# Two elementwise products of a state-space scan on another engine, and the first layer's modulation by wide matrix products

## The chip, the cores and the metric

The program runs on one core of a Trainium2 chip. The core has a matrix engine (TensorE, PE in the profile, with its weight loads as PEld), a vector engine (VectorE, DVE), an engine for activations and scaled copies (ScalarE, ACT), a general engine (GpSimd, POOL) and a queue that issues the DMAs (SyncE, SP). The metric is the device time of one execution in microseconds (us), lower is better. A comparison of two versions of this kernel can tell about 0.3% from no change.

## The reference

Two layers of a diffusion backbone over 1024 latent tokens (x) and 256 context tokens, width 1024, fp32 in and out. Each layer does:

```python
mod = silu(c) @ w_mod[l] + b_mod[l]            # once for x (c), once for the context (c_ctx)
sh, sc, g = split(mod, 3)
h = rmsnorm(x, norm_w) * (1 + sc) + sh         # adaLN
fu, fg, q, k, v, ag, z, xbc, dt, gates = split(h @ w_in[l])
y_f = (fourier_mix(fu) * silu(fg)) @ w_of      # 2-D Fourier branch
y_a = (diff_attention(q, k, v) * silu(ag)) @ w_oa
y_s = rmsnorm(ssd(xbc, dt) * silu(z)) @ w_os   # bidirectional state-space (SSD) branch
x = x + g * ((sigmoid(g0)*y_f + sigmoid(g1)*y_a + sigmoid(g2)*y_s) @ w_out[l])
```

and the SSD branch, for chunks c of 128 tokens, 2 groups of 4 heads of 64 channels, state 128, both directions:

```python
y[c] = (C B^T * decay mask * dt) x + (C @ H_fwd[c]) * ecs_f + (C @ H_bwd[c]) * ecs_b + d_skip * x
H[c+1] = H[c] * etot[c] + B^T @ (x * w)        # the same backwards for H_bwd
```

The result is a final rmsnorm of x.

## The kernel before

All products of the model run on TensorE. Activations and weights are split into a high and a low fp16 part, so one product of the model is three fp16 matmuls of up to 512 columns; small products of the SSD scan, the transposes and the modulation are fp32, which the profile shows as two PE records for one matmul. Weights come as 512 KB halves into a ring of two raw buffers, are squared on ACT, given a power-of-two scale through a one-column product on PE, and are split by ACT and DVE into the w buffers. Activations live in 28 slots of SBUF (`ar`).

The builder writes the program as five cooperating threads: p (the projections of h), m (the three branches one after another: Fourier, attention, SSD), f (the merges with gates and w_out, and the norm of the next layer), e (the gates of the last branch) and g (the modulation of layer 1 and the residual gates). Every instruction goes to a list scheduler (`Scheduler.add` and `Scheduler.step`, lines 235 and 330), which keeps a planned clock for each engine, with a planned duration (`cost`, line 214) and planned delays between engines, and gives each engine that becomes free the ready instruction with the best priority. The priority is the number in order of creation, minus a bias by thread (`BIAS`, line 47). `AHEAD` says how many instructions a thread may have pending, `HOLD` when ACT and DVE may wait a little for a more urgent instruction, and the threads draw on common slots, PSUM banks and w buffers. The order that comes out is fixed at build time: on the chip each engine goes through its list in order and waits where an operand is late. So a change of a table, of a planned duration or of a dependency reorders the whole program.

All instructions are emitted at line 400, so the profile's rows have L400 throughout, and are told apart by engine, operation and tile.

The parts that the change touches:

- `mod0` (line 735) forms shift and scale of layer 0, before anything else can start. The modulation weights come as 16 tiles of 128 x 1024 (`in_wm`). For each tile 8 matmuls take 128 columns of the tile as stationary operand and the two columns of `cs` (silu of c and of c_ctx) as moving operand, all summed into 32 columns of one PSUM bank. Between the tiles the loads of x and of the first weights are issued. Then `modT` is read out, `mod_finish` makes `ab` of it, and `norm_T` transposes the first four tiles of x and applies `ab`; the first fp16 product needs all of that.
- `ssd_scan` (line 1280) runs per layer and group. Backwards first, 9 steps (`step`, line 1292): xw = x * w on DVE, one product on PE, then `new = old * etot` and `new += product`, both on DVE. Then for each chunk forwards: the mask from `rows`, C B^T on PE, ACT and DVE make the weighted mask, four products of 64 columns (`y`), C times both states (`y2`), and the sum on DVE, which begins with the skip product `acc = x * d_skip` and goes on with `acc += y` and so on. Then one `step` of H.
- When both groups are through, `ssd_out` norms and transposes the result to `zS`, and `merge_last` and `finish` follow, which need it whole.

Of the kernel before, what the change touches and what calls it, by code (L numbers as in the profile page):

```python
# [15 lines left out]
ALU = mybir.AluOpType  # L16
# [27 lines left out]
NSLOT = 28  # L44
NW = 8
RAW = 2
BIAS = {'m': 1200, 'p': 300, 'w': 1000, 'f': 0, 'e': -50000, 'g': -100000}
AHEAD = {'m': 120, 'p': 120, 'f': 40, 'e': 27, 'g': 6}
MAXB = {'m': 4, 'p': 3, 'f': 3, 'e': 1, 'w': 1, 'g': 1}
LEAST = (1, 1)  # L50
WLIM = {'p': 2, 'f': 4, 'e': 1}
# [1 line left out]
CAP = {'F': 5, 'S': 10, 'A': 9}  # L53
RES = 2
BOR, BMAX = 2, 4
HOLD = 0.25
X_AT, W_AT = 4, 7
G_AFTER = 'fu2'
F_START, F_FIN = 1000, 300
C_FIN = (2, 2)  # L60
# [90 lines left out]
class Scheduler:  # L151
# [66 lines left out]
    def cost(self, eng, name, outs, ins, kw, args):  # L218
        n = max(a.free_size() for a in outs + ins)
        if eng == 'PE':  # L220
            if name != 'matmul':
                return args[1].free_size() * NS_PE * 2 + 3.0
            n = args[2].free_size() * NS_PE
            return max(3.0 + n, 25.0) if ESIZE[ins[0].dtype] == 2 else max(4 * n + 3.0, 223.0)
        if eng == 'ACT':
            aps = len(ins) - 1
            return (51 if ins[0].space == PSUM else 93) + n * NS_ACT + 93 * (aps + len(outs) - 1)
        if eng == 'DVE':
            fast = name == 'tensor_copy' or name == 'tensor_scalar'
            fast = fast and all(a.space != PSUM for a in outs + ins)  # L230
            scal = sum(a.free_size() == 1 for a in ins[1:]) if name in ('tensor_scalar', 'scalar_tensor_tensor') else 0
            return 68 + n * NS_DVE * (0.5 if fast else 1) + 61 * scal
        return 60.0 if name != 'tensor_copy' else 150.0 + 2 * n

    def add(self, eng, name, fn, args, kw):
        o = Op()
# [181 lines left out]
class Builder:  # L418
# [173 lines left out]
    def prefetch(self, want=None):  # L592

        idle = self.block.get('f') in {(l, 'z' + b) for l in range(2) for b in ORDER[1:]}
        for k in 'pef' if idle else 'pfe':
            while self.wnext[k] and self.wnext[k][0][0] < (self.layers if k == 'p' else min(self.layers, self.flayer + 1)):
                l, name = self.wnext[k][0]
                ahead = k == 'p' and self.wnext['f'] and l > self.wnext['f'][0][0]
                left = k == 'f' and self.wnext['e'] and self.wnext['e'][0][0] == l
                lim = 1 if ahead else (0 if idle else 2) if left else WLIM[k] if (self.fetch_p if k == 'p' else self.fetch_f) else 0  # L600
                wo = name in ('wo0', 'wo1')
                need = 2 + max(0, self.later) + (0 if (l, name) == want else BOR if wo and self.wborrow < BMAX else 99)
                borrow = (ahead or wo) and len(self.free) >= need
                if not ahead and name[:2] != 'wo' and not self.later and (k != 'p' or l <= self.flayer) and self.spare < 4 and len(self.free) >= 6:
                    borrow = True
                if self.whold[k] >= lim or len(self.wfree) < 2 and not borrow:
                    break
                self.fetch(k)
# [126 lines left out]
    def mod0(self, L):  # L735

        nc, V = self.nc, self.nc.vector
        t = self.mm(True)
        nc.bias['w'] = 0
        zero = self.small(32)  # L740
        nc.gpsimd.memset(zero, 0.0)
        for k in range(8):
            for part in (1, 0):
                yield ('slots', 1)
                s = self.alloc()
                nc.sync.dma_start(s.v(1024), self.A['wm'][0, part, k])
                if k == 0 and part:
                    self.mul(t[:, 0:32], s.v(1024)[:, 0:128], zero, True, False)
                for b in range(8):
                    c = 16 * part + 2 * b  # L750
                    self.mul(t[:, c:c + 2], s.v(1024)[:, b * 128:b * 128 + 128], self.cs[:, k], False, k == 7 and not part and b == 7)
                s.drop()
            if k == 1:
                self.consts()
# [4 lines left out]
            if k == W_AT:  # L759
                self.fetch_p = True  # L760
                self.prefetch()
        modT = self.cst.tile([128, 16, 2], F32, name="modT0")
        V.tensor_tensor(modT, t[:, :32].rearrange("p (b s) -> p b s", s=2), self.pv[0][:, 0:16].unsqueeze(2).to_broadcast([128, 16, 2]), ALU.add)
        nc.close('p', True)
        self.mod_finish(L, modT)
        nc.bias['w'] = BIAS['w']
# [509 lines left out]
    def ssd_scan(self, L, g):  # L1276
# [14 lines left out]
        def step(c, dr, old, new):  # L1291
# [4 lines left out]
            if old is None:  # L1296
                V.tensor_copy(new, p[:, :256])
            else:
                V.tensor_tensor(new.rearrange(h4, q=64), old.rearrange(h4, q=64), bc4(L.etot, c, dr), ALU.mult)
                V.tensor_tensor(new, new, p[:, :256], ALU.add)  # L1300

        order = [9, 8, 7, 6, 5, 4, 3, 2, 1, 0]
# [4 lines left out]
        for c in [8, 9, 0, 1, 2, 3, 4, 5, 6, 7]:  # L1307
            if c < L.nt:
# [30 lines left out]
                if c != 9:  # L1339
                    self.mul(y2[:, 0:256], G.CT.v(1284)[:, o:o + 128], hb[c], True, True)  # L1340
                acc, t = self.scr()[:, :256], self.scr()[:, :256]
                V.tensor_tensor(acc.rearrange(h4, q=64), G.x[c].rearrange(h4, q=64),
                                b[:, 32 + g * 4:36 + g * 4].unsqueeze(2).to_broadcast([128, 4, 64]), ALU.mult)
                V.tensor_tensor(acc, acc, y[:, 0:256], ALU.add)
                for dr in range(2):
# [743 lines left out]
```

## Time and profile before

| | us |
|---|---|
| median of 3 runs | 2589.57 (2583.79 to 2592.41) |
| the profiled execution | 2585.78 |
| its span, first to last instruction | 2584.0 |
| PE busy | 2486.6 (96%) |
| DVE busy | 1821.3 (70%) |
| ACT busy | 1268.0 (49%) |
| POOL busy | 47.5 (2%) |

The program has no stage in which PE has nothing to do by design, so what counts is where PE stands idle, and where it runs at the lower of its two clocks. Both are read by stretches: idle is the length of a stretch minus PE's busy time in it, and PEclk is the clock that was granted (1.00 is 2.4 GHz, 0.50 is 1.2 GHz). Three stretches stand out from an even picture: the first 76 us, some 73 us near 2400 us, which are the last chunks of the second group's scan in layer 1 and `ssd_out`, and the last 14 us.

### The profile page before, as it was taken

What the parts mean: (1) busy time and instruction counts of PE and PEld (TensorE: products, weight loads), DVE (VectorE), ACT (ScalarE), POOL (GpSimd) and SP (SyncE); (2) the same over time, 40 slices, a digit from 0 to 9 for tenths busy, and PEclk for the clock granted to TensorE, in tenths of its full rate; (3) what the DMA queues carried; (4) which work ended last, traced back from release to release, by engine and by line L of the source; (5) the groups of instructions that cost most, each with busy time, mean ns of one, the idle gap of its engine ahead of it and who ended that gap; (6) DMA issues with size and microseconds to landing.
All of it is one profiled execution on the core that took longest, in us unless ns stands there. A gap on an engine that the chain in (4) does not pass through costs nothing. (4 is left out here: it accounts for less than half of the span.)

```text
span 2584.0 us, 42400 instructions
## 1 busy us (share of the span) xinstructions
PE 2486.6 (96%) x16800; PEld 1572.5 (61%) x16800; DVE 1821.3 (70%) x3823; ACT 1268.0 (49%) x2398; POOL 47.5 (2%) x93
## 2 busy tenths in 40 slices
PE   9999999999999999999999999999999999998698
PEld 9655665657565665575587556555655556556467
DVE  1868565687877898468956775776477768748766
ACT  2654453545655564456513654554464656446221
POOL 0200000000000000000000000000000000000000
PEclk9999999999999999999999999999999999999699
DMA  6132243354433334213722122434343423232331
GB/s 250 50 131 77 65 101 82 80 148 111 112 78 89 131 116 142 87 55 119 286 79 99 57 90 66 109 94 98 82 122 88 100 95 106 78 102 87 131 131 66
DMA packets 256979, 270.61 MB, mean 105 GB/s; under 512 B 181062, under 2 KB 191110, under 8 KB 256780
## 3 DMA queue, kind: packets, MB, share of 16 engines
q1 hardware_dynamic: 256780, 267.89, 34.5%
q8 instruction: 132, 2.16, 0.3%
q14 instruction: 67, 0.55, 0.1%
HBM read 178.02 MB, written 36.88 MB: 83 GB/s over the span
## 5 line engine op out<-in xcount | busy, mean ns | idle before, releaser
L400 PE MATMUL ps<-ar,w 128*128 128x512 f16 (+1 forms) x7296 | 1476.8, 355 | 3.7 <-ACT w L400 2.7
L400 PEld LDWEIGHTS <-w 128*128 128x128 f16 x7296 | 708.7, 98 | 649.6 <-issue 17.0
L400 PEld LDWEIGHTS <-ar 128*128 128x128 f16 x8000 | 648.9, 98 | 231.3 <-issue 26.4
L400 PE MATMUL ps<-ar,ar 128*128 128x128 f16 (+4 forms) x4564 | 564.7, 274 | 31.2 <-DVE ar L400 18.4
L400 PE MATMUL ps<-w,ar 128*128 128x256 f16 x3312 | 396.0, 273 | 0.0
L400 ACT ACTIVATE ar<-ps,s1m,qksc 128x1280 f32<-128x1280 f32 (+1 forms) x144 | 190.1, 1320 | 194.4 <-DVE s1m L400 158.0
L400 DVE TENSOR_REDUCE s1m<-ps 128x1 f32<-128x1280 f32 (+1 forms) x144 | 196.9, 1368 | 101.8 <-PE ps L400 91.0
L400 ACT ACTIVATE w<-raw 128x1024 f16<-128x1024 f32 x147 | 154.5, 1051 | 180.9 <-PE ps L400 105.5
L400 ACT ACTIVATE ar<-ar 128x1280 f16<-128x1280 f32 (+5 forms) x140 | 138.1, 987 | 104.6 <-DVE ar L400 103.0
L400 DVE TENSOR_TENSOR ar<-ar,ar 128x1280 f16<-128x1280 f32 (+3 forms) x116 | 123.4, 1064 | 9.3 <-ACT ar L400 9.0
L400 DVE SCALAR_TENSOR_TENSOR ar<-ar,pv,ar 128x1284 f32<-128x1284 f32 (+1 forms) x64 | 97.1, 1517 | 32.9 <-ACT ar L400 32.3
L400 ACT ACTIVATE ar<-ps 128x128 f32<-128x128 f32 (+5 forms) x192 | 67.3, 386 | 104.6 <-PE ps L400 103.6
L400 ACT ACTIVATE ar<-ps,ds 128x512 f32<-128x512 f32 (+1 forms) x86 | 53.9, 627 | 114.4 <-PE ps L400 114.3
L400 DVE SCALAR_TENSOR_TENSOR ar<-ar,s1m,ar 128x1280 f32<-128x1280 f32 (+1 forms) x72 | 103.1, 1432 | 0.0
L400 ACT ACTIVATE ar<-ar,ar 128x128 f32<-128x128 f32 x288 | 90.1, 388 | 22.8 <-DMA ar<-rows 21.7
L400 ACT ACTIVATE w<-raw,s1p 128x1024 f16<-128x1024 f32 x72 | 79.0, 1138 | 33.9 <-DVE s1p L400 33.7
L400 DVE SCALAR_TENSOR_TENSOR w<-raw,s1p,w 128x1024 f16<-128x1024 f32 x72 | 89.8, 1279 | 7.9 <-ACT w L400 7.7
L400 PE MATMUL ps<-k,ar 128*128 128x128 f32 (+1 forms) x492 | 79.3, 289 | 15.5 <-DVE ar L400 14.7
L400 DVE SCALAR_TENSOR_TENSOR w<-raw,s1f,w 128x1024 f16<-128x1024 f32 x65 | 81.4, 1279 | 9.8 <-ACT w L400 9.8
L400 PEld LDWEIGHTS ps<-k,ar 128*128 128x128 f32 x492 | 63.1, 157 | 38.2 <-DVE ar L400 23.3
L400 DVE SCALAR_TENSOR_TENSOR scrf<-ps,ds,ar 128x256 f32<-128x256 f32 x72 | 34.7, 482 | 72.6 <-PE ps L400 72.3
L400 PEld LDWEIGHTS ps<-ar,ar 128*128 128x128 f32 x428 | 67.0, 206 | 29.7 <-DVE ar L400 20.8
(218 smaller groups left out, 2157.0 us busy)
## 6 DMA issues: line engine op xcount, KB each, us to landing
raw<-in_wt SPq DMA_DIRECT2D x160, 512.0 KB, 4.7
ar<-in_wm SPq DMA_DIRECT2D x48, 512.0 KB, 6.4
ar<-rows SPq DMA_DIRECT2D x36, 512.0 KB, 4.5
yp<-scrf SPq DMA_DIRECT2D x64, 256.0 KB, 2.2
ar<-in_x SPq DMA_DIRECT2D x20, 512.0 KB, 9.5
gs<-scre SPq DMA_DIRECT2D x32, 256.0 KB, 2.0
scrf<-yp SPq DMA_DIRECT2D x32, 256.0 KB, 2.7
ar<-ar SPq DMA_DIRECT2D x32, 160.0 KB, 2.8
```

Of the source, the lines that this page charges most:

```text
L400: o.fn(*(place(a) for a in o.args), **{k: place(a) for k, a in o.kw.items()})
```

## The change

The decay of the old state (`new = old * etot`, in `step`) and the skip product (`acc = x * d_skip`) are issued on GpSimd. The planner prices a GpSimd product of two tensors like its copies. `mod0` turns its products round: the two columns of `cs` become the stationary operand and 512 columns of the weight tile the moving one, so 32 matmuls of 512 columns give two rows in four PSUM banks; ACT and DVE copy them out, and 16 small transposes bring them to the old layout. The loads of x and of the first weights move up by one step of the loop. Numbers of the planner change: the biases, the pending limit of thread m, `HOLD`, and the count of free slots from which weights may borrow one.

```diff
-BIAS = {'m': 1200, 'p': 300, 'w': 1000, 'f': 0, 'e': -50000, 'g': -100000}
+BIAS = {'m': 1000, 'p': 400, 'w': 400, 'f': 0, 'e': -50000, 'g': -100000}
...
-X_AT, W_AT = 4, 7
+X_AT, W_AT = 3, 6
...
-        return 60.0 if name != 'tensor_copy' else 150.0 + 2 * n
+        return 60.0 if name not in ('tensor_copy', 'tensor_tensor') else 150.0 + 2 * n
...
     def mod0(self, L):
...
-        t = self.mm(True)
+        row = [self.alloc(), self.alloc()]
+        p = [[self.mm(True), self.mm(True)] for _ in range(2)]
...
-                for b in range(8):
-                    c = 16 * part + 2 * b
-                    self.mul(t[:, c:c + 2], s.v(1024)[:, b * 128:b * 128 + 128], self.cs[:, k], False, k == 7 and not part and b == 7)
+                for i in range(2):
+                    self.mul(p[part][i][:2], self.cs[:, k], s.v(1024)[:, i * 512:i * 512 + 512], k == 0, k == 7)
...
+        t = self.mm(True)
+        for part in (1, 0):
+            for i in range(2):
+                r = row[part].v(1024)[:2, i * 512:i * 512 + 512]
+                if i:
+                    V.tensor_copy(r, p[part][i][:2])
+                else:
+                    nc.scalar.activation(r, p[part][i][:2], AF.Copy)
+            for b in range(8):
+                nc.tensor.transpose(t[:, 16 * part + 2 * b:16 * part + 2 * b + 2], row[part].v(1024)[:2, b * 128:b * 128 + 128], self.ident[:2, :2])
         modT = self.cst.tile([128, 16, 2], F32, name="modT0")
...
             else:
-                V.tensor_tensor(new.rearrange(h4, q=64), old.rearrange(h4, q=64), bc4(L.etot, c, dr), ALU.mult)
+                nc.gpsimd.tensor_tensor(new.rearrange(h4, q=64), old.rearrange(h4, q=64), bc4(L.etot, c, dr), ALU.mult)
                 V.tensor_tensor(new, new, p[:, :256], ALU.add)
...
                 acc, t = self.scr()[:, :256], self.scr()[:, :256]
-                V.tensor_tensor(acc.rearrange(h4, q=64), G.x[c].rearrange(h4, q=64),
+                nc.gpsimd.tensor_tensor(acc.rearrange(h4, q=64), G.x[c].rearrange(h4, q=64),
                                 b[:, 32 + g * 4:36 + g * 4].unsqueeze(2).to_broadcast([128, 4, 64]), ALU.mult)
                 V.tensor_tensor(acc, acc, y[:, 0:256], ALU.add)
```

The order of instructions shows the moves. First ACT at the start of the program, before (`raw` is a half of the first weight, `w` its buffer, `nss` the sums of squares of x, `ab` the scale and shift made of the modulation):

```order
7 L400 ACTIVATE w_92,s1p<-raw 128x1024
8 L400 ACTIVATE w_93,s1p<-raw 128x1024
9 L400 ACTIVATE scrf,nss_144<-ar_68 128x1024
10 L400 ACTIVATE scrf,nss_144<-ar_69 128x1024
11 L400 ACTIVATE w_92<-raw,s1p 128x1024
```

and ACT at the same place now:

```order
7 L400 ACTIVATE w_92,s1p<-raw 128x1024
8 L400 ACTIVATE ar_75<-ps 2x512
9 L400 ACTIVATE w_93,s1p<-raw 128x1024
10 L400 ACTIVATE scrf,nss_144<-ar_68 128x1024
11 L400 ACTIVATE ar_74<-ps 2x512
12 L400 ACTIVATE scrf,nss_144<-ar_69 128x1024
13 L400 ACTIVATE scrf,nss_144<-ar_70 128x1024
14 L400 ACTIVATE w_92<-raw,s1p 128x1024
```

The two copies of modulation rows stand behind the squares of the first weight's halves and of one tile of x of the second group. Next PE in the last chunks of the last scan (layer 1, second group), before (128x64 is `y`, H and the next row `y2`, `scrm` the product of a state step, 128x128 is C B^T of the next chunk):

```order
29305 L400 MATMUL ps<-ar_71,ar_86 128x64 x4
29306 L400 MATMUL ps<-H,ar_79 128x256
29307 L400 MATMUL ps<-ar_76,ar_79 128x256
29308 L400 MATMUL ps<-scrm,ar_74 128x256
29309 L400 MATMUL ps<-ar_79,ar_85 128x128
29310 L400 MATMUL ps<-ar_71,ar_64 128x64 x4
29311 L400 MATMUL ps<-H,ar_79 128x256
```

and PE there now, the last chunk but one and the start of the next:

```order
29090 L400 MATMUL ps<-ar_79,ar_87 128x64 x4
29091 L400 MATMUL ps<-H,ar_86 128x256
29092 L400 MATMUL ps<-ar_72,ar_86 128x256
29093 L400 LDWEIGHTS w_94
29094 L400 MATMUL ps<-ar_89,w_94 128x512
...
29118 L400 MATMUL ps<-ar_85,w_96 128x512
29119 L400 MATMUL ps<-scrm,ar_78 128x256
29120 L400 MATMUL ps<-ar_86,ar_70 128x128
29121 L400 LDWEIGHTS w_96
29122 L400 MATMUL ps<-ar_85,w_96 128x512
...
29150 L400 MATMUL ps<-ar_74,w_94 128x512
29151 L400 MATMUL ps<-ar_79,ar_82 128x64 x4
```

Between `y2` and the state step stand 13 fp16 matmuls of 512 columns now, and 15 between C B^T and the next `y`, where nothing stood before; they belong to merges, and it is alike in all of this scan's last five chunks. Last DVE in the last chunk of that scan, before:

```order
3184 L400 TENSOR_TENSOR scrm<-ar_71,ar_89 128x256
3185 L400 TENSOR_TENSOR scrm<-ar_71,bc_295 128x256
3186 L400 TENSOR_TENSOR H<-H,ps 128x256
3187 L400 TENSOR_TENSOR scrm<-ps,k_140 128x128 x2
3188 L400 SCALAR_TENSOR_TENSOR ar_73<-scrm,ar_89,ar_73 128x128 x4
3189 L400 TENSOR_TENSOR ar_73<-ar_73 128x512
3190 L400 TENSOR_TENSOR scrm<-scrm,ps 128x256
```

and the end of POOL's list now, in the same scan:

```order
160 L400 TENSOR_TENSOR H<-H,ar_73 128x256
161 L400 TENSOR_TENSOR scrm<-ar_79,bc_217 128x256
162 L400 TENSOR_TENSOR H<-H,ar_73 128x256
163 L400 TENSOR_TENSOR scrm<-ar_79,bc_217 128x256
164 L2093 UNCONDITIONAL_BRANCH
```

The skip product (`scrm<-...,bc`) and the decay (`H<-H,ar`) have left DVE's list and alternate on POOL, where nothing else stands between them.

## Rows read from the trace of the kernel before

**Rows 1.** The page's first part, PE: busy us, share of the span, instructions.

```profile
PE 2486.6 (96%) x16800; PEld 1572.5 (61%) x16800; DVE 1821.3 (70%) x3823; ACT 1268.0 (49%) x2398; POOL 47.5 (2%) x93
```

**Rows 2.** Windows: stretch, length, busy by engine, PEclk, DMA share, GB/s.

```profile
5.00:60.00 55.00, 54.96 (x258) 54.99 (x259) 5.12 (x18) 9.19 (x16) 0.00 (x0) 1.00 0.70 277
60.00:76.00 16.00, 11.83 (x64) 10.53 (x65) 14.42 (x43) 11.10 (x17) 6.37 (x8) 0.79 0.19 65
100.00:2300.00 2200.00, 2154.56 (x14768) 1324.00 (x14766) 1582.29 (x3210) 1128.58 (x2120) 32.36 (x71) 1.00 0.35 102
2300.00:2376.00 76.00, 75.55 (x460) 47.46 (x458) 54.65 (x116) 41.80 (x95) 0.00 (x0) 1.00 0.28 90
2376.00:2449.00 73.00, 40.90 (x166) 29.00 (x165) 53.20 (x160) 29.89 (x80) 0.00 (x0) 0.65 0.34 115
2570.00:2584.00 14.00, 3.83 (x36) 3.19 (x33) 8.24 (x29) 1.95 (x4) 0.00 (x0) 0.73 0.28 112
```

**Rows 3.** Timeline of the first 80 us: start, duration, engine, operation, [idle before, releaser].

```profile
5.46 54.75 PE L400 MATMUL ps<-cs,ar 128*128 128x2 f32 x256
...
34.19 1.06 ACT L400 ACTIVATE w<-raw 128x1024 f16<-128x1024 f32 x1 [7.70 <-DMA raw<-in_wt]
35.15 0.19 ACT L400 ACTIVATION_READ_ACCUMULATOR w<-raw 128x1 f32 x1
...
60.25 0.19 DVE L400 TENSOR_TENSOR modT<-ps,pv 128x32 f32<-128x32 f32 x1 [23.45 <-PE ps L400]
...
75.80 3.83 PE L400 MATMUL ps<-ar,w 128*128 128x512 f16 x17
```

**Rows 4.** Windows of the first 40 us; the last column is the DMAs' GB/s.

```profile
0.00:20.00 20.00, 14.96 (x71) 14.99 (x71) 0.77 (x4) 1.50 (x2) 0.33 (x5) 1.00 0.83 320
20.00:40.00 20.00, 20.00 (x95) 20.00 (x96) 4.71 (x16) 9.19 (x16) 0.00 (x0) 1.00 1.03 412
```

**Rows 5.** Groups on PE, whole span: count | busy us, mean ns | idle before.

```profile
L400 PE MATMUL ps<-cs,ar 128*128 128x2 f32 x256 | 54.8, 352 | 0.0
```

**Rows 6.** Timeline of PE near 1052 us, wide fp32 products.

```profile
1052.30 1.88 PE L400 MATMUL ps<-ar,k 128*1 128x512 f32 x4
```

**Rows 7.** Groups on PE from 2376 to 2449 us.

```profile
L400 PE MATMUL ps<-ar,ar 128*128 128x64 f32 x48 | 10.1, 378 | 14.1 <-DVE ar L400 13.7 <-issue 0.4
L400 PE MATMUL ps<-ar,ar 128*128 128x512 f16 x36 | 10.0, 431 | 0.0
```

**Rows 8.** Groups on PE from 2330 to 2376 us.

```profile
L400 PE MATMUL ps<-ar,ar 128*128 128x64 f32 x16 | 2.1, 272 | 0.0
```

**Rows 9.** Groups on PE from 2449 to 2510 us.

```profile
L400 PE MATMUL ps<-ar,w 128*128 128x512 f16 x190 | 41.2, 379 | 0.0
```

**Rows 10.** Timeline of PE from 2428 to 2447 us.

```profile
2428.87 1.19 PE L400 MATMUL ps<-scrm,ar 128*128 128x256 f32 x2 [2.96 <-DVE scrm L400]
...
2433.30 1.97 PE L400 MATMUL ps<-ar,ar 128*128 128x64 f32 x8 [2.80 <-DVE ar L400]
...
2442.93 3.67 PE L400 MATMUL ps<-k,ar 128*128 128x128 f32 x16 [5.85 <-DVE ar L400]
```

**Rows 11.** Groups on POOL, whole span.

```profile
L400 POOL COPY ar<-ar 64x1280 f16<-64x1280 f16 x8 | 10.6, 1322 | 1465.6 <-DMA ar<-ar 946.5 <-DVE ar L400 265.1 <-DVE s1m L400 137.5
L400 POOL CAST ar<-scrf 128x512 f16<-128x512 f32 x8 | 7.3, 942 | 3.8 <-ACT scrf L400 3.8
```

**Rows 12.** Groups on DVE, whole span.

```profile
L400 DVE TENSOR_TENSOR ar<-ar 128x512 f32<-128x512 f32 x88 | 59.1, 686 | 7.8 <-ACT ar L400 6.8
...
L400 DVE TENSOR_TENSOR scrm<-ar,bc 128x256 f32<-128x256 f32 x36 | 15.0, 417 | 2.3 <-ACT scrm L400 2.2
...
L400 DVE TENSOR_TENSOR ar<-ar,ar 128x256 f32<-128x256 f32 x32 | 13.3, 416 | 0.1
L400 DVE TENSOR_TENSOR H<-H,ar 128x256 f32<-128x256 f32 x32 | 13.3, 415 | 0.0
...
L400 DVE TENSOR_TENSOR ar<-scrf,ar 128x512 f16<-128x512 f32 x8 | 8.0, 1031 | 1.5 <-POOL ar L400 1.5
```

More of the change, by code (lines that the diff above doesn't have):

```diff
@@ L46 @@
 RAW = 2
-BIAS = {'m': 1200, 'p': 300, 'w': 1000, 'f': 0, 'e': -50000, 'g': -100000}
-AHEAD = {'m': 120, 'p': 120, 'f': 40, 'e': 27, 'g': 6}
+BIAS = {'m': 1000, 'p': 400, 'w': 400, 'f': 0, 'e': -50000, 'g': -100000}
+AHEAD = {'m': 140, 'p': 120, 'f': 40, 'e': 27, 'g': 6}
 MAXB = {'m': 4, 'p': 3, 'f': 3, 'e': 1, 'w': 1, 'g': 1}
@@ L55 @@
 BOR, BMAX = 2, 4
-HOLD = 0.25
-X_AT, W_AT = 4, 7
+HOLD = 0.35
+X_AT, W_AT = 3, 6
 G_AFTER = 'fu2'
@@ L603, in prefetch @@
                 borrow = (ahead or wo) and len(self.free) >= need
-                if not ahead and name[:2] != 'wo' and not self.later and (k != 'p' or l <= self.flayer) and self.spare < 4 and len(self.free) >= 6:
+                if not ahead and name[:2] != 'wo' and not self.later and (k != 'p' or l <= self.flayer) and self.spare < 4 and len(self.free) >= 5:
                     borrow = True
@@ L737, in mod0 @@
         nc, V = self.nc, self.nc.vector
-        t = self.mm(True)
+        row = [self.alloc(), self.alloc()]
+        p = [[self.mm(True), self.mm(True)] for _ in range(2)]
         nc.bias['w'] = 0
-        zero = self.small(32)
-        nc.gpsimd.memset(zero, 0.0)
         for k in range(8):
@@ L746, in mod0 @@
                 nc.sync.dma_start(s.v(1024), self.A['wm'][0, part, k])
-                if k == 0 and part:
-                    self.mul(t[:, 0:32], s.v(1024)[:, 0:128], zero, True, False)
-                for b in range(8):
-                    c = 16 * part + 2 * b
-                    self.mul(t[:, c:c + 2], s.v(1024)[:, b * 128:b * 128 + 128], self.cs[:, k], False, k == 7 and not part and b == 7)
+                for i in range(2):
+                    self.mul(p[part][i][:2], self.cs[:, k], s.v(1024)[:, i * 512:i * 512 + 512], k == 0, k == 7)
                 s.drop()
@@ L761, in mod0 @@
                 self.prefetch()
+        t = self.mm(True)
[8 more added lines that the diff above has]
+                nc.tensor.transpose(t[:, 16 * part + 2 * b:16 * part + 2 * b + 2], row[part].v(1024)[:2, b * 128:b * 128 + 128], self.ident[:2, :2])
         modT = self.cst.tile([128, 16, 2], F32, name="modT0")
         V.tensor_tensor(modT, t[:, :32].rearrange("p (b s) -> p b s", s=2), self.pv[0][:, 0:16].unsqueeze(2).to_broadcast([128, 16, 2]), ALU.add)
+        for r in row:
+            r.drop()
         nc.close('p', True)
```

## The prediction

> **What bounds the kernel now.** I read the page's first part, then windows over the span, then the timeline where a window stands out. PE is busy 2486.6 of 2584.0 us [rows 1], so the other engines matter only where PE waits for them. The windows show where that is [rows 2]. In the 2200 us from 100 to 2300 PE is idle 45.4 us in all, in pieces; from 2300 to 2376 it is idle 0.45. From 2376 to 2449 it is idle 32.1 of 73 us and runs at a mean clock of 0.65. From 60 to 76 it is idle 4.2, at 0.79, and in the last 14 us 10.2. From 5 to 60 us PE counts as busy throughout, but with one thing only: the 256 records of the modulation's narrow products, end to end in 54.75 us, and `modT` is formed right behind them at 60.25, the first fp16 product at 75.80 [rows 3]. So an end of the program that comes earlier must come from the opening, from the 73 us near 2400, or from the 45 us spread between.
>
> The busy opening hides its clock. PEclk says 1.00 there, but one record takes 54.8/256 = 214 ns with a mean latency of 352 ns [rows 5]. The records of `y`, with the same 128-column fp32 weight load and a short moving side, take 10.1/48 = 210 ns (latency 378) where the granted clock is 0.65 [rows 7], and 2.1/16 = 131 ns (latency 272) where it is 1.00 [rows 8]. I read the opening as run at 1.2 GHz, whatever the column says.
>
> **The opening.** Removed: 128 narrow products, and the work from 5.0 to 60.2 us. Added: 32 products of 512 columns, 16 small transposes, four copies. Four wide fp32 records take 1.88 us at full clock [rows 6], 0.94 us for a product of two records, and twice that, 1.88, at half clock. PE starts cold; the clock rose in the stretch near 2447 while PE did transposes without a gap from 2442.93 on for 3.67 us [rows 10], so I take the first two products at half clock and thirty at full: 2 x 1.88 + 30 x 0.94 = 32.0 us, end at 37.0. Are the tiles there? Ahead of the last one stand 16 tiles, 4 of x and 0.26 MB of constants, 10.7 MB, as before; 320 GB/s over 20 us and 412 GB/s after that [rows 4] bring them by 6.4 MB + 4.3/0.412, at 30.5 us. So PE sets 37.0, not the DMAs.
>
> Behind it a new wait: the two copies on ACT stand in its queue behind the squares of the first weight's halves and of one tile of x. The first square starts at 34.19, released by its DMA, and takes 1.06 + 0.19 us [rows 3]. Three of them and two copies: a copy of 512 columns is not in these rows, the 1024-column operation at 1.06 us is above it, so 0.55 each (between 0.3 and 1.06): 34.19 + 3.75 + 1.1 = 39.0. ACT is later than PE by two us. Then 8 transposes, 16 records with the same weight load as `y`, at 131 to 214 ns, 2.1 to 3.4 us, and the read-out: `modT` at 42, against 60.25. **Term: -18 us**, if what follows `modT` still takes its 15.5 us to the first fp16 product. It should: x and the first weights are issued behind the same bytes, and the path there is transposes, ACT, POOL and DVE, none of which the change touches; the squares of x that now fall behind `modT` are about two, 2.5 us at worst. Bounds: -22 (no cold product, copies hidden) to +8 (below).
>
> The Trainium skill, "TensorE: Matmul & The Clock Gate", section "Part 1: The HAM clock gate", says that throttled is the default state and activity releases it. The trace agrees only for some activity: here 55 us without a gap did not release it [rows 3, 5].
>
> **The tail of the last scan.** In the last chunks of layer 1's second scan PE had nothing but the scan: it waited 2.80 us for the mask before `y` and 2.96 us for the state step in each chunk, and then 5.85 us for the norm before the first transpose [rows 10]. Half speed costs on top: the 48 records of `y` would take 6.3 in place of 10.1 us at 131 ns [rows 8], the 36 fp16 matmuls 7.8 in place of 10.0 at 41.2/190 = 217 ns [rows 9], and of the other 21 us of busy time I put some 3 to this. So the stretch holds about 33 us of work at full clock, and 73 - 33 = 40 us are lost in it. The order now has 13 fp16 matmuls in the one gap and 15 in the other, 2.8 and 3.3 us at 217 ns, in each of the last five chunks, and 27 of them (5.9 us) behind the last `y2`. That nearly equals the gaps. That a filled scan keeps pace is shown by the stretch ahead: from 2300 to 2376, partly the same scan with merges between, PE was idle 0.45 us, with DVE busy 54.65 of 76 [rows 2]. What is late next: DVE's part of the chunk, with the merges' own products now in its queue. I leave 1 us per chunk and 2 to 3 us at the norm, 8 in all. **Term: -32 us** (from -38 with every gap closed to -10, if the merges' operands on DVE delay each chunk by some 5 us, as much as the gaps were).
>
> **The two products on GpSimd.** DVE loses 36 skip products at 417 ns and 64 decays at 415, 15.0 + 13.3 + 13.3 = 41.6 us [rows 12], nearly all of it beside PE's work: below 0.5 us per chunk of it is on the path, and I count nothing for it. Added: 100 products of two tensors on POOL. The trace has none. From below, 0.42 us, DVE's own time; from above 1.32 us, the copy of 1280 columns; nearest is the cast of 512 columns at 0.94 [rows 11], and since the shape has half the columns and two inputs I take that, 0.9. Their cover: a decay is wanted one chunk later forwards, some 10 us, and the skip product after the mask and `y`; both hide. Backwards there is no such slack: 32 of the decays stand in chains of eight, where the next add waits for POOL and everything behind it in DVE's list waits too. A link grows from two products of 0.42 us to 0.9 + 0.42 and two crossings; I put a crossing at 0.2 from POOL's small share in such waits: some 0.9 us more. Most of this is in the plan, since the planner prices and orders it; what the plan misses I put at a tenth of a link's growth to half of it, on PE 0 to +14 us, and take +4 with what the reordering does to the other 45 us of idle time (which could shrink as well, by 10). DVE also slows beside POOL: its products of 512 columns take 1031 ns behind POOL's casts and 686 elsewhere [rows 12]. 100 overlaps of 0.35 us are 35 us of DVE time, which gives back most of the 41.6. **Term: +4 us.**
>
> The Trainium skill, "GPSIMD Engine Reference", section "4.1 Engine selection", advises VectorE for elementwise work and calls GpSimd about two times slower for two inputs. That ratio on the 417 ns would be an estimate of 0.83 us, and the sum stays as it is.
>
> **The rest.** The last 14 us keep their chain of norm and output. The edit of biases, `AHEAD` and `HOLD` has no duration of its own; it shows only in the order.
>
> **Sum.** Against the profiled execution: 2585.8 - 18 - 32 + 4 = 2539.8. The runs' median is 2589.57, 3.8 above that execution; the saving of 46 us carried to the median is 2543.6, and I forecast 2543.
>
> **The rivals.**
> - The fill is robbed from elsewhere. The merges that now stand in the tail must have stood earlier in layer 1, where they covered something; if that shows, some 20 of the 32 us come back as waits between 1500 and 2300. For it: PE's idle time there was small because work was at hand. Against it: the planner had none left over before, so its own gaps must have shrunk. Time: 2563.
> - The wide products stay at 1.2 GHz, as the narrow ones did. Then 32 x 1.88 = 60 us, end at 65, and the transposes at 214 ns: `modT` near 69, +8 in place of -18. For it: 55 us of work that did not raise the clock [rows 5]. Against it: there the moving side was 2 columns, here 512, like the matmuls that raise it elsewhere. Time: 2569.
> - Slower: the links through GpSimd. If a product on POOL takes the 1.32 us of the upper bound, slows against DVE by 1031/686 [rows 12], and crossings come twice, a link grows by 1.9 us; if 32 links backwards and as many forwards hold DVE's list that long while PE waits, 64 x 0.9 = 58 us or more. From 46/64 = 0.72 us of PE time per link on, the gain is gone. Against it: PE has merges and gates beside the scans, and forwards the slack is long. Time: 2601.
> - The change does next to nothing: the opening's gain turns into waiting for the first weights, and the tail's filler is late itself because its weights are. ACT waits 7.7 us for the first of them [rows 3]. Time: 2588.
>
> **How the numbers follow.** Forecast 0.54, robbed fill 0.18, cold wide products 0.13, slower 0.08, nothing 0.07. The forecast's own range is 2525 to 2562. For 8 in 10 I reach up past the second and third case, which end at 2563 and 2569 with some 10 us of spread, and leave out slower and nothing: 2519 to 2581, the low end being the tail wholly closed and 10 us off the spread idle time. Within 0.3% means 2582 to 2597, about what a measurement here can tell from no change. Faster than that: the first three cases, 0.85; same: 0.07; slower: 0.08.
>
> **What would show it.** In the profile of the changed kernel: the wide products end near 37 us at some 0.47 us per record, `modT` stands near 42 and the first fp16 product near 57; fp16 matmuls between `y2` and the state steps in the last scan, with PE idle under 10 us from there to the last norm and the clock at 1.00; POOL's products near 0.9 us; idle time in the middle between 35 and 60 us. Wrong would be: records of 0.9 us in the opening, waits of PE for DVE of 2 us and more in the last chunks, or waits of DVE for POOL that sum to over 50 us with PE idle behind them.

## The result and the profile after

The changed kernel takes 2555.24 us (median of 4 runs, 2549.55 to 2557.58) beside 2586.83 of the kernel before on the same chip: a ratio of 0.9872, 95% interval 0.9847 to 0.9898. Timed again on another chip the ratio was 0.9896 (0.9879 to 0.9913). So it is 1.0 to 1.3% faster, some 12 us less than forecast. Its profiled execution takes 2554.75 us with a span of 2553.0, 31.0 us less than that of before.

First the page's first part, then windows of the kernel after (columns as in [rows 1] and [rows 2]):

```profile
PE 2457.3 (96%) x16622; PEld 1520.4 (60%) x16622; DVE 1805.7 (71%) x3725; ACT 1272.5 (50%) x2400; POOL 116.7 (5%) x192
```

```profile
100.00:2300.00 2200.00, 2133.37 (x14556) 1313.75 (x14554) 1557.07 (x3084) 1118.51 (x2095) 86.17 (x147) 0.99 0.35 100
700.00:900.00 200.00, 191.41 (x1451) 115.05 (x1450) 150.69 (x249) 103.47 (x183) 0.98 (x13) 0.98 0.45 128
1190.00:1250.00 60.00, 49.09 (x279) 32.93 (x278) 50.69 (x146) 31.03 (x76) 3.60 (x6) 0.89 0.62 208
1500.00:2300.00 800.00, 775.21 (x5088) 446.06 (x5087) 552.29 (x986) 425.29 (x753) 32.70 (x58) 0.99 0.34 91
2300.00:2440.00 140.00, 135.07 (x761) 80.27 (x760) 120.95 (x290) 79.33 (x183) 15.46 (x24) 1.00 0.41 141
```

The same stretches of the kernel before, as far as [rows 2] doesn't have them:

```profile
700.00:900.00 200.00, 196.09 (x1556) 122.02 (x1555) 150.99 (x261) 110.58 (x208) 1.00 (x12) 1.00 0.37 104
1190.00:1250.00 60.00, 58.87 (x333) 35.07 (x332) 54.82 (x154) 35.91 (x76) 0.00 (x0) 0.97 0.43 151
1500.00:2300.00 800.00, 784.47 (x5179) 450.83 (x5178) 560.16 (x1032) 422.99 (x756) 15.67 (x34) 1.00 0.35 93
2300.00:2440.00 140.00, 110.38 (x589) 71.00 (x586) 99.06 (x235) 67.78 (x166) 0.00 (x0) 0.84 0.30 99
```

Idle is the length minus PE's busy time. From 2300 to 2440 us, which holds the last chunks of layer 1's second scan in both kernels, it fell from 29.6 to 4.9 us, and the clock rose from 0.84 to 1.00. From 100 to 2300 it rose from 45.4 [rows 2] to 66.6, by 21.2 us: by 10.0 up to 1260 us, where layer 0's last scan is over in both kernels, and by 11.2 behind that. In the rows, 700 to 900 has 4.7 more, 1190 to 1250 has 9.8, and 1500 to 2300 has 9.3; between them it also shrank.

The opening after, timeline (columns as in [rows 3], which it answers to):

```profile
6.37 15.87 PE L400 MATMUL ps<-ar,cs 128*2 128x512 f32 x32 [6.37 <-DMA ar<-in_wm]
22.56 13.89 PE L400 MATMUL ps<-ar,cs 128*2 128x512 f32 x32 [0.33 <-DMA ar<-in_wm]
...
33.92 0.59 ACT L400 ACTIVATE ar<-ps 2x512 f32<-2x512 f32 x1
...
36.49 0.57 ACT L400 ACTIVATE ar<-ps 2x512 f32<-2x512 f32 x1
...
37.80 0.19 DVE L400 TENSOR_TENSOR modT<-ps,pv 128x32 f32<-128x32 f32 x1 [0.63 <-PE ps L400]
...
53.33 2.75 PE L400 MATMUL ps<-ar,w 128*128 128x512 f16 x12 [0.31 <-ACT scrf L400]
```

The wide products end at 36.4 us, the last 32 records at 0.43 us each; `modT` stands at 37.80 in place of 60.25, and the first fp16 product at 53.33 in place of 75.80: **22.5 us gained**. In the last scan, which answers to [rows 10], PE's timeline now reads:

```profile
2350.77 0.67 PE L400 MATMUL ps<-scrm,ar 128*128 128x256 f32 x2
...
2352.39 2.54 PE L400 MATMUL ps<-ar,w 128*128 128x512 f16 x11
2355.86 1.08 PE L400 MATMUL ps<-ar,ar 128*128 128x64 f32 x8 [0.93 <-ACT ar L400]
...
2357.69 3.40 PE L400 MATMUL ps<-ar,w 128*128 128x512 f16 x15
2361.04 0.67 PE L400 MATMUL ps<-scrm,ar 128*128 128x256 f32 x2
```

Between `y2` and the state step, and before `y`, stand fp16 matmuls, and the waits of 2.96 and 2.80 us are gone: of the 40 us lost there at most 5 are left, **about 35 gained** (an estimate, since the 40 is one). Then 22.5 + 35 - 31 = **26 us are given back**. 21 of them are the new idle time from 100 to 2300 us. The rest is about what the lower clock can cost there. Between 100 and 2300 us PE is busy at a granted clock of 0.50 for 18.9 us in the kernel before and for 29.7 in the one after; if half of such time is lost, the 10.8 us more cost 5, an estimate from above. The largest hole is at the end of layer 0's second scan, on PE:

```profile
1221.80 1.72 PE L400 MATMUL ps<-ar,ar 128*128 128x64 f32 x8 [2.22 <-DVE ar L400]
1223.31 1.17 PE L400 MATMUL ps<-H,ar 128*128 128x256 f32 x2
1224.27 1.06 PE L400 MATMUL ps<-ar,ar 128*128 128x256 f32 x2
1225.13 0.21 PE L400 MATMUL ps<-b16m,ones 128*128 128x1 bf16 x1
1231.19 3.68 PE L400 MATMUL ps<-k,ar 128*128 128x128 f32 x16 [5.85 <-DVE ar L400]
```

It is the bare tail of [rows 10] with the same 5.85 us before the transposes, one layer earlier. In the kernel before, 30 fp16 matmuls stood in this place, right behind the one-column product:

```profile
1230.61 6.63 PE L400 MATMUL ps<-ar,w 128*128 128x512 f16 x30
1237.16 0.44 PE L400 MATMUL ps<-k,ar 128*128 128x128 f32 x2
```

GpSimd's part: its three groups of products, and below them what VectorE waited for GpSimd (us in total, times, longest).

```profile
L400 POOL TENSOR_TENSOR scrm<-ar,bc 128x256 f32<-128x256 f32 x36 | 26.3, 731 | 238.1 <-ACT scrm L400 238.1
L400 POOL TENSOR_TENSOR ar<-ar,ar 128x256 f32<-128x256 f32 x32 | 22.4, 700 | 376.8 <-DVE ar L400 371.3 <-PE ps L400 4.9 <-DVE s1f L400 0.6
L400 POOL TENSOR_TENSOR H<-H,ar 128x256 f32<-128x256 f32 x32 | 21.3, 664 | 11.3 <-DVE H L400 11.1
```

```profile
DVE H L400 <- POOL scrm L400: 7.5, 9, 0.9
DVE ar L400 <- POOL ar L400: 6.4, 11, 0.8
DVE H L400 <- POOL ar L400: 1.8, 2, 0.9
```

A product takes 0.66 to 0.73 us, 1.6 to 1.75 times VectorE's 0.415 to 0.417 [rows 12], and VectorE waits 15.7 us in these three groups (1.5 of such waits stood in the second one before), never over 0.9. The Trainium skill, "GPSIMD Engine Reference", section "4.1 Engine selection", calls GpSimd about two times slower for two inputs. The trace has somewhat less.

### The profile page after: what moved, and what is told of

Read it like the earlier page. It is cut to its first block, busy times and chain, and to the rows that moved or that the text cites. A ratio compares the mean times of both kernels' runs of the same rounds, so it can differ in the third digit from the quotient of the medians.

```text
span 2553.0 us, 42118 instructions
## 1 busy us (share of the span) xinstructions
PE 2457.3 (96%) x16622; PEld 1520.4 (60%) x16622; DVE 1805.7 (71%) x3725; ACT 1272.5 (50%) x2400; POOL 116.7 (5%) x192
## 5 line engine op out<-in xcount | busy, mean ns | idle before, releaser
L400 PE MATMUL ps<-ar,w 128*128 128x512 f16 (+1 forms) x7128 | 1444.6, 355 | 4.7 <-ACT w L400 1.9
L400 PE MATMUL ps<-ar,ar 128*128 128x128 f16 (+5 forms) x4492 | 569.1, 278 | 32.2 <-DMA ar<-ar 11.9
L400 PE MATMUL ps<-w,ar 128*128 128x256 f16 x3552 | 427.9, 273 | 0.9 <-DVE scrp L400 0.9
L400 ACT ACTIVATE ar<-ar 128x1280 f16<-128x1280 f32 (+4 forms) x140 | 138.1, 987 | 101.1 <-DVE ar L400 98.0
L400 ACT ACTIVATE ar<-ps 128x128 f32<-128x128 f32 (+4 forms) x194 | 68.4, 387 | 125.8 <-PE ps L400 124.4
L400 DVE TENSOR_TENSOR ar<-ar,ar 128x1280 f16<-128x1280 f32 (+2 forms) x84 | 110.1, 1312 | 11.0 <-ACT ar L400 10.4
L400 PE MATMUL ps<-k,ar 128*128 128x128 f32 (+2 forms) x508 | 80.3, 284 | 19.1 <-DVE ar L400 18.6
L400 DVE SCALAR_TENSOR_TENSOR w<-raw,s1f,w 128x1024 f16<-128x1024 f32 x66 | 83.8, 1288 | 11.6 <-ACT w L400 11.5
L400 PEld LDWEIGHTS ps<-k,ar 128*128 128x128 f32 (+1 forms) x508 | 63.7, 154 | 46.1 <-DVE ar L400 28.4
L400 DVE SCALAR_TENSOR_TENSOR ar<-ar,ps 128x512 f32<-128x512 f32 (+1 forms) x116 | 64.1, 561 | 36.2 <-ACT ar L400 25.5
L400 DVE TENSOR_TENSOR ar<-ar 128x512 f32<-128x512 f32 (+4 forms) x142 | 78.5, 575 | 5.1 <-ACT ar L400 3.7
```

The source lines that it names most:

```text
L400: o.fn(*(place(a) for a in o.args), **{k: place(a) for k, a in o.kw.items()})
```

## The experiments

Theory: the opening's gain belongs to the wide products, the tail's to the planner's numbers, nothing to GpSimd, and what is given back belongs to the order. Rivals: GpSimd's products cost the middle; or the tail needs VectorE relieved. Filler below is work of other threads, fp16 matmuls above all, that PE's list has between a branch's own instructions, and a hole is a place without it, where PE waits.

For all runs but warm_narrow, of which only the opening is read, idle time of PE in us, in one profiled execution each: from 100 to 2300; in the 200 us from 700, where layer 0's attention ends; in 70 us around the last `y` of layer 0's second scan (45 before its start, 25 behind); and in 105 us around that of layer 1's (80 and 25).

| kernel | ratio to before (95%) | 100-2300 | 700-900 | layer 0's end | layer 1's end |
|---|---|---|---|---|---|
| before | 1 | 45.4 | 3.9 | 4.6 | 32.3 |
| after | 0.9872 (0.9847-0.9898) | 66.6 | 8.6 | 11.1 | 2.5 |
| num_only | 1.0115 (1.0100-1.0131) | 92.1 | 16.8 | 12.8 | 0.7 |
| wide_only | 1.0224 (1.0207-1.0241) | 112.4 | 41.3 | 17.7 | 20.4 |
| pool_only | 0.9976 (0.9967-0.9985) | 53.5 | 4.2 | 1.3 | 20.9 |
| no_pool | 0.9864 (0.9851-0.9878) | 63.8 | 7.8 | 14.5 | 0.9 |
| held_vector | 0.9912 (0.9898-0.9926) | 76.0 | 9.0 | 11.5 | 2.9 |
| held_gpsimd | 1.0003 (0.9994-1.0012) | 45.7 | 4.0 | 4.4 | 29.7 |
| bias_1190 | 1.0170 (1.0151-1.0188) | 101.6 | 18.6 | 20.4 | 7.4 |
| held_wide | 0.9921 (0.9906-0.9936) | 44.2 | 5.1 | 4.9 | 30.9 |
| four_filled | 0.9833 (0.9819-0.9848) | 62.4 | 11.7 | 1.7 | 1.4 |
| four_filled_vector | 0.9857 (0.9840-0.9873) | 62.3 | 12.2 | 1.1 | 3.7 |
| changed_again | 0.9896 (0.9879-0.9913) | 66.1 | 7.5 | 11.7 | 2.4 |

**One part alone.** num_only:

```diff
-BIAS = {'m': 1200, 'p': 300, 'w': 1000, ...
-AHEAD = {'m': 120, ...
+BIAS = {'m': 1000, 'p': 400, 'w': 400, ...
+AHEAD = {'m': 140, ...
...
-HOLD = 0.25
+HOLD = 0.35
...
-    if not ahead and ... and len(self.free) >= 6:
+    if not ahead and ... and len(self.free) >= 5:
```

> The kernel before with the planner's numbers alone (BIAS, AHEAD, HOLD and the free-slot condition); both products stay on VectorE and layer 0's modulation stays narrow. My theory, that the numbers fill the last scan: in layer 1's second scan the order now has some 29 fp16 matmuls between one chunk's y and the next in every chunk, as the changed kernel has, so PE idles under 4 us from there to the norm and some 36 us go; the opening stays (first fp16 product near 75.8 us); the middle gives back 10 to 25 us, above all at the end of layer 0's second scan, where the order has chunks with 1.3 and 4.3 us of filler. Time 2562 to 2577. Rival, that the tail needs the products off VectorE: the filler stands there but PE waits for VectorE in each chunk, 2 us or more, and the time is 2580 to 2595.

Measured 2610.47 us, 29 slower. Half of my theory held: the numbers alone fill the last scan. The size of what comes back did not: 47 us of new idle time, of which 13 at 700 to 900 and 8 at layer 0's end. Windows of num_only:

```profile
700.00:900.00 200.00, 183.21 (x1383) 107.60 (x1382) 150.86 (x255) 99.30 (x176) 4.26 (x15) 0.97 0.43 120
1240.00:1310.00 70.00, 57.16 (x341) 38.34 (x340) 63.42 (x178) 31.71 (x78) 0.00 (x0) 0.95 0.44 154
2365.00:2470.00 105.00, 104.29 (x590) 63.98 (x589) 98.07 (x270) 58.89 (x154) 0.00 (x0) 1.00 0.39 135
```

wide_only: `mod0` of the changed kernel and `X_AT, W_AT = 3, 6`, the rest as before.

> The kernel before with the wide modulation products alone, and the loads of x and of the first weights issued one tile earlier. My theory: the first fp16 product comes 22.5 us earlier, as in the changed kernel, at 53.3 us; the last scan is filled only in its first chunks (the order has 3.4, 3.8, 6.4 and 0 us of fp16 work in the last four), so about a third of its 40 us comes back; time 2545 to 2570, and 2566 if the tail gives nothing. Rival, that the opening's gain is lost in waits for the first weights behind it: the same first fp16 product, but 10 us and more of new idle time between 53 and 200 us and a time above 2575.

Measured 2640.21 us, 59 slower: above the rival's 2575, but not by what it named (4.7 us of idle time from 53 to 200). The opening did gain (the wide products end at 36.7 us, the first fp16 product comes at 53.58). But from 740 to 830 us, where attention ends, PE had no filler and waited for the softmax; the window, and the two largest waits of PE from 690 to 860 us:

```profile
740.00:830.00 90.00, 53.43 (x339) 31.41 (x337) 72.79 (x111) 34.74 (x67) 0.11 (x1) 0.73 0.50 136
```

```profile
PE ps L400 <- ACT ar L400: 31.8, 10, 6.5
PE ps L400 <- DVE ar L400: 4.3, 1, 4.3
```

pool_only: the two products on GpSimd and their planned price, the rest as before.

> The kernel before with the two products on GpSimd alone (with their planned price). My theory, that GpSimd itself is worth nothing either way: opening as before, the last scan filled by two thirds (the order has 2.1, 6.4, 3.9 and 0 us of fp16 work in the last four chunks), VectorE waits for GpSimd some 16 us in sum but PE not; time 2565 to 2590 by the order alone. Rival, that the crossings to GpSimd and VectorE's slower two-input operations beside it cost the middle: PE idle time between 100 and 2300 us rises from 45 to over 65 us and the time is 2590 to 2610.

Measured 2574.91 us, as the theory had it. The last scan is filled by a third, from 32.3 to 20.9 us of idle time, where I had two thirds. The numbers and the wide products each lose alone (1.2 and 2.2%), and no_pool, which comes next, has just the two together and gains; the table's effects don't add.

**One part undone.** no_pool: the changed kernel with both products on VectorE, without their price.

> The changed kernel with both products back on VectorE and without their price, planned anew: wide modulation and the planner's numbers stay. My theory: opening at 53.3 us and the last scan filled as in the changed kernel (the same 6.0 to 6.6 us of fp16 work per chunk), GpSimd worth nothing by itself; time 2545 to 2565, within 0.4% of the changed kernel's 2555. Rival one, that GpSimd's products are what costs the middle its 28 us: time 2525 to 2540. Rival two, that the tail needs VectorE relieved: PE waits for VectorE in the last chunks and the time is 2575 to 2590.

Measured 2545.46 us, 0.9864: not slower than the changed kernel. The whole gain is there without GpSimd, the filled scan too (0.9 us idle), and the middle is no better (63.8 us of idle time beside 66.6). Both rivals fall on this order; the next runs ask on the two others.

**Order held.** A planned order can be kept while one instruction is issued elsewhere: in held_vector the products are planned for GpSimd and issued to VectorE, in held_gpsimd the other way round.

```diff
+self.other = Queue(self, 'POOL', nc.vector)     # held_gpsimd: ('DVE', nc.gpsimd)
-nc.gpsimd.tensor_tensor(new..., old..., ...)
+nc.other.tensor_tensor(new..., old..., ...)
```

> The changed kernel with its order held: every engine's list is planned as in the changed kernel, but the 100 products planned for GpSimd are issued to VectorE at the places where they stand. No replanning, so only the engine differs. My theory, that GpSimd is worth nothing on the chip either: 2547 to 2562 where the changed kernel takes 2550, VectorE busy about 40 us more, PE idle within 10 us of the changed kernel's 95.7. Rival one, that relief of VectorE is what keeps the filled scans going: PE waits for VectorE in the scans and the time is 2570 to 2590. Rival two, that the crossings to GpSimd and the slower two-input operations beside it cost the middle: 2530 to 2542.

> The kernel before with its order held, and the 100 products issued to GpSimd at the places where they stood for VectorE. My theory, no price of their own: 2575 to 2588 beside the 2581 of the kernel before, the unfilled last scan a little shorter or longer by at most 5 us since there each chunk's chain is bare. Rival one, the crossings: in the bare chunks each chain grows by 1 to 1.5 us and elsewhere PE waits behind VectorE, 2595 and more. Rival two, relief: 2560 to 2570.

Measured 2561.11 us (0.9912) and 2582.06 us (1.0003). On the order of before the engine makes no difference. On that of after, VectorE came out 4 to 10 us slower, by the changed kernel's second and first ratio (0.0016 and 0.0040 of 2583 us); the second interval (0.9879 to 0.9913) overlaps, so that it is slower at all is not shown. PE's idle time rose by 10.5 us over the span (2560.0 - 2453.8 beside 95.7), at the edge of the 10 that I allowed. VectorE is busy 1829.0 us in held_vector, 23.3 more than after, though 41.6 us of products moved. Of the 18.3 us between, some 11 are VectorE's other instructions, which take longer in after: the sum of all its records, the products included, is 2000.1 us in held_vector and 1968.9 in after, 31.2 less. The others are records that overlap the next one, which the busy time counts once. The group that lost most, in after and then in held_vector:

```profile
L400 DVE TENSOR_TENSOR scrm<-ar,ar 128x256 f32<-128x256 f32 x72 | 32.0, 471 | 1.7 <-PE ps L400 0.6
L400 DVE TENSOR_TENSOR scrm<-ar,ar 128x256 f32<-128x256 f32 x72 | 29.0, 420 | 1.5 <-PE ps L400 0.4
```

**The order alone.** bias_1190:

```diff
-BIAS = {'m': 1200, ...
+BIAS = {'m': 1190, ...
```

> The kernel before with one number of the table changed by less than a hundredth, BIAS of thread m from 1200 to 1190. Nothing that the program computes and no planned duration differs; only the order does. In the order layer 1's last scan is now filled in every chunk (6.2 us of fp16 work or more, in place of 0.9, 5.1, 0, 0, 0), and it is layer 0's second scan whose last chunks are bare (1.3 and 0 us). My theory, that the hole moves from scan to scan with the order and the numbers of the change have no merit that any other number has not: PE idles under 5 us in layer 1's last scan, 15 us or more at the end of layer 0's, and the time is 2585 to 2625, as far from the kernel before as the whole change is. Rival, that the order is stable against such an edit and the tail's gain is a property of the change's numbers: 2575 to 2587, or 2545 if the hole just goes.

Measured 2624.52 us: 42 us slower by an edit that changes no instruction. Layer 1's last scan is filled (7.4 us idle in place of 32.3), and the same hole stands in layer 0. That hole is not the whole loss: of 56 us of new idle time from 100 to 2300 it has 16, and 700 to 900 has 15. PE's timeline of bias_1190, to be read beside [rows 10]:

```profile
1282.01 1.97 PE L400 MATMUL ps<-ar,ar 128*128 128x64 f32 x8 [3.38 <-DVE ar L400]
...
1288.76 1.19 PE L400 MATMUL ps<-scrm,ar 128*128 128x256 f32 x2 [2.97 <-ACT scrm L400]
...
1293.18 1.97 PE L400 MATMUL ps<-ar,ar 128*128 128x64 f32 x8 [2.81 <-DVE ar L400]
...
1302.84 3.68 PE L400 MATMUL ps<-k,ar 128*128 128x128 f32 x16 [5.87 <-DVE ar L400]
```

**The wide products by themselves.** held_wide plans the narrow products and issues wide ones:

```diff
+class Wide:
+    def matmul(self, out, a, c, **kw):          # called for each of 8 planned products of a tile
+        if self.n == 1:
+            for i in range(2):
+                nc.tensor.real.matmul(nc.ps[4 + 2 * part + i][:2], c, self.tile[:, i * 512:...], ...)
+        ... behind the last: 4 row copies, 16 transposes into t
```

> The kernel before with its order held and the wide modulation products in the place of the narrow ones: planned as narrow, issued as 32 wide products, four row copies and 16 small transposes (rows kept in two idle weight buffers). Behind the opening every engine has the list of the kernel before. My theory, that the wide products are a gain of their own and what wide_only lost came from its order alone: first fp16 product at 53 to 56 us in place of 75.8, everything behind it as before with the bare last scan too, time 20 to 23 us under the kernel before, 2557 to 2563 beside 2581. Rival, that a shorter opening is paid later on the chip, because loads and weights are then the limit: under 10 us of gain, with PE waiting for DMAs or ACT between 55 and 200 us.

Measured 2564.16 us beside 2584.67: 20.5 us, and behind the opening nothing moved. The loads stand where they stood before, and the first fp16 product comes at 54.02, so moving them up is worth 0.7 us of the 22.5. The same wide products thus lose 59 us where the program is planned anew and gain 20.5 where it is not. And since held_wide has a ratio of 0.9921 beside 0.9872 and 0.9896, all the rest of the change, tail included, adds 6 to 13 us. Windows of held_wide, the second with the bare tail still in it:

```profile
100.00:2300.00 2200.00, 2155.78 (x14701) 1321.18 (x14700) 1580.38 (x3180) 1125.39 (x2111) 32.77 (x71) 1.00 0.35 102
2325.00:2430.00 105.00, 74.08 (x366) 50.71 (x364) 83.49 (x232) 49.77 (x131) 0.00 (x0) 0.76 0.39 132
```

warm_narrow asks whether the narrow products could have been fast.

```diff
...
+V.memset(warm.v(1024)[:, 0:512], 0.0)
+for _ in range(6):
+    self.mul(t[:, 0:512], warm.v(1024)[:, 0:128], warm.v(1024)[:, 0:512], True, True)
...
```

> The kernel before, narrow modulation products, with six wide fp32 products of zeros (512 columns) put ahead of them on PE, which write a bank that is overwritten later. Asked is the opening alone: does PE's rate depend on the operation, or on the clock it is left at? Theory, that the narrow products don't hold the clock up: the zeros run at 0.85 us per record and then 0.43, the narrow records behind them fall back to 214 ns, and the first fp16 product comes at 78 to 82 us, later than before by the zeros. Rival, that 214 ns was only the state in which they started: 131 ns per record throughout, and the first fp16 product at 58 to 64 us, which would give more than half of the wide products' gain without them.

Only its opening is read; the six products replan all that follows, and the 2707.48 us are of one run. PE's timeline, then windows:

```profile
1.45 7.38 PE L400 MATMUL ps<-ar 128*128 128x512 f32 x12 [1.45 <-DVE ar L400]
...
8.80 51.61 PE L400 MATMUL ps<-cs,ar 128*128 128x2 f32 x256
...
77.05 1.71 PE L400 MATMUL ps<-ar,w 128*128 128x512 f16 x7
```

```profile
5.00:10.00 5.00, 5.00 (x22) 3.01 (x20) 0.23 (x1) 0.00 (x0) 0.00 (x0) 1.00 1.02 414
10.00:15.00 5.00, 5.00 (x35) 5.00 (x35) 0.10 (x1) 0.00 (x0) 0.00 (x0) 0.73 0.83 325
15.00:20.00 5.00, 5.00 (x25) 5.00 (x25) 0.09 (x1) 0.00 (x0) 0.00 (x0) 0.50 0.92 371
```

The zeros leave the clock at 1.00; the first narrow products run at it, and then it falls to 0.50 and stays there, with PE busy all the time. The first fp16 product comes at 77.05, 1.3 us later than before. So the low clock comes with the narrow products themselves, whatever it was ahead of them.

**A version that beats both.** four_filled, chosen so that PE's list has fp16 matmuls in every chunk of all four scans (counted between one `y` and the next):

```diff
-AHEAD = {'m': 140, ...
+AHEAD = {'m': 160, ...
...
-LEAST = (1, 1)
+LEAST = (1, 2)
...
-X_AT, W_AT = 3, 6
+X_AT, W_AT = 4, 7
...
-    if not ahead and ... and len(self.free) >= 5:
+    if not ahead and ... and len(self.free) >= 6:
```

> The changed kernel with four numbers of the planner changed again, chosen from the order alone so that no scan has a bare chunk: LEAST (1, 2), AHEAD of m 160, loads after tiles 4 and 7, the free-slot condition at 6. In the order each chunk of all four scans has 4.5 us of fp16 work or more, 6.2 and more at the ends of both layers' second scans (the changed kernel has 5.1, 4.5 and then nothing at the end of layer 0's). My theory, that the time is the sum of the holes left: the 14 us that the changed kernel loses between 1190 and 1250 go to under 5, opening and last scan stay as they are, time 2530 to 2546. Rival, that holes only move: as much is lost elsewhere in layer 0 or 1, 2550 to 2565.

> The order of four_filled held, with the 100 products issued to VectorE in place of GpSimd. held_vector was 0.4% slower than the changed kernel, with intervals that nearly touch; this asks again on another order. Theory, that relief of VectorE is worth a few microseconds where all scans are filled: 5 to 14 us above four_filled, PE's waits for VectorE and ACT longer by as much. Rival, that GpSimd is worth nothing and the 0.4% was particular to that order: within 4 us of four_filled.

Measured 2541.53 us (0.9833) and 2545.41 us (0.9857). Windows of four_filled at the two ends:

```profile
1190.00:1250.00 60.00, 59.01 (x355) 36.67 (x354) 53.04 (x149) 28.99 (x58) 3.91 (x5) 1.00 0.53 191
2305.00:2410.00 105.00, 103.54 (x571) 61.51 (x570) 90.72 (x241) 59.29 (x151) 14.70 (x24) 1.00 0.38 127
```

Against 0.9872 and 0.9896 of the changed kernel it is faster by 0.4 to 0.6%, with the first interval just touching. The hole in layer 0 is closed, as the theory had it, by 9.4 us; but idle time from 100 to 2300 fell by only 4.2, so 5 us came back elsewhere, 3 of them at 700 to 900, and that speaks in part for the rival. The question on GpSimd stays open: 3.9 us with overlapping intervals is the rival's side of my line.

The changed kernel timed again, unedited:

> The changed kernel itself, unedited, timed once more against the kernel before, since its first ratio, 0.9872 with 0.9847 to 0.9898, touches the intervals of held_vector and four_filled. My theory, that GpSimd relieves VectorE by a few microseconds in this order and that four_filled is faster by the hole at the end of layer 0's second scan: a ratio of 0.986 to 0.989, so above four_filled's 0.9833 and below held_vector's 0.9912. Rival, that the three differ by the spread of chips alone: a ratio below 0.985, or above 0.990.

Measured 2559.59 us, 0.9896, at the theory's upper edge and just past it. Its profile, with a span of 2558.0 us, is 5.0 longer than the first one's; idle time from 100 to 2300 is the same (66.1), but PE is busy there at the clock of 0.50 for 39.8 us and not 29.7. So two executions of one kernel differ here by as much as sets it apart from held_vector by the second ratio.

## Why the prediction was right, and where it was not

**The opening** was right, with a term too small: -18 forecast, -22.5 in the trace, -20.5 by held_wide. PE's end was right (37.0, measured 36.4). The copies on ACT were not: I let both queue behind three squares and end at 39.0. The first stands behind one square, at 33.92 us, the second behind all three, at 36.49, right as PE ends, because the first square came at 32.79 in place of 34.19. The reading of 1.2 GHz against the profile's own column holds (warm_narrow). The rival of cold wide products falls: of the first 32 records some five took 0.85 us (15.87 against 13.89 us), the rest 0.43.

**The tail** was right in place and nearly in size (-32, about -35). I had left open which edit fills it. It is the order that the planner's numbers make: num_only has 0.7 us of idle time there, pool_only 20.9; and these numbers have no merit of their own, since bias_1190 fills it with another (7.4). My 1 us per chunk for VectorE was a little much. Two sums of mine are off by little: 40.9 us less 3.8, 2.2 and 3 leaves 31.9 us of work and not 33, so 41 us were lost; and the low end of the 8-in-10 range, by what I name for it (8 and 10 us under 2543), would be 2525 and not 2519.

**GpSimd**: +4 was wrong in sign if anything. In none of the three held pairs did it cost PE measurable time (0, -4 and -4 to -10 us held, and no loss without it in no_pool), and the rival of links that hold VectorE's list falls: waits of 0.9 us at most. I had its product at 0.9 us, measured 0.66 to 0.73. That VectorE slows beside it held, but with some 11 us (held_vector) where I had 35, and the two rows that I set side by side for it, 1031 and 686 ns, differ in form.

**The step that failed** is the last part of that term, "what the reordering does to the other 45 us of idle time", put at a few us, and the argument against the first rival, that the planner's own gaps "must have shrunk". The middle gave back some 26 us, with 66.6 us of idle time where I had 35 to 60. It is the rival's size (20), and only in part its place: of the 21.2 us of new idle time 9.3 lie between 1500 and 2300, where the rival had its waits, and 10.0 up to 1260 us, in layer 0, which shares no work with the tail. Whether the 9.3 are the merges that now stand in the tail is not shown; for it speaks that num_only, no_pool and four_filled, whose last scan is filled, have 27.7, 19.0 and 25.1 us of idle time there beside 15.5 in the kernel before, against it that wide_only, whose scan is not, has 31.0. Of the part in layer 0, bias_1190 shows the cause: the hole at a scan's end comes and goes with the order, in either layer, at 11 to 32 us of idle time apiece. It could have been read ahead of the run. In PE's list of the changed kernel nothing but a one-column product stands between layer 0's last `y2` and the transposes of the norm; I counted filler in the last scan only. Which number of the table opens the hole at 1221 us is not settled.

## What to carry to other kernels

Where one program-wide plan sets the order, an edit has two prices, its own and that of the new order, and the second can be larger than the first with either sign: hold the order to measure the first, and look through every place of the same kind in the new list for the second. A part that loses when tried alone (here the wide products, by 2.2%) can be worth 0.8% for itself. And a stretch in which the matrix engine is busy throughout can still be at half its clock: compare the time per record with that of the same kind elsewhere.

## What the hardware showed that was not expected

Being busy did not keep the clock up: with PE busy in 5.00 of 5.00 us the granted clock went from 1.00 to 0.50 under products with 2 moving columns, and stayed there to their end. In the changed kernel it rose under 512-column ones, whose records went from 0.85 to 0.43 us. The Trainium skill, "TensorE: Matmul & The Clock Gate", section "Part 1: The HAM clock gate", ties the clock to how busy the engine has been. The rows here agree with that only in part, since PE's busy time in the profile was full while the clock fell. Also, the column of the clock reads 1.00 from the start to its first change: before's narrow records took 214 ns under "1.00" [rows 2, 5], and warm_narrow's took 200 ns (25 in 5.00 us) under 0.50.

GpSimd's products slow some of VectorE's instructions and not others. In after, the 53 products `scrm<-ar,ar` that no GpSimd instruction overlaps took 421 ns in the mean; 15 that were overlapped for more than half of their time took 664, up to 836. The sums that read one operand from PSUM (`H<-H,ps`, same shape) took 419 ns without and 417 with such an overlap (14 and 11 of them).
